# Second and third feed-forward of a two-layer diffusion backbone: third chunk of four inner tiles, projected by seven block products

## The chip, the core and the metric

One core of one Trainium2 chip runs the whole inference step as one program. The metric is the device time of that program in microseconds (us); lower is better. Three runs of the kernel before took 2325.58, 2327.49 and 2329.98 us; the median is 2327.49 us.

## The reference

640 token rows (512 latent ones, 128 context ones) of width 1024 go through two layers. Each layer is a feed-forward, a mixer and a second feed-forward, all in float32:

```python
def ffn_sub(x, g, shift, scale, gate, w_in, w_out):
    h = modulate(rms_norm(x, g), shift, scale)
    a, b = jnp.split(h @ w_in, 2, axis=-1)
    return x + gate * (FFN_RESIDUAL * ((jax.nn.silu(a) * b) @ w_out))
```

The inner width is 2816, which is 22 tiles of 128. `shift`, `scale` and `gate` come from `silu(c) @ w_mod + b_mod`, a product of one vector for each of the two token groups with a 1024 by 9216 matrix for each layer. The mixer of layer 0 holds pooling and neighbourhood attention, that of layer 1 grouped-query attention.

## The kernel before

Activations are kept transposed: `x[m]`, m = 0 to 7, holds 128 of the 1024 features by 640 tokens. Tokens are handled in two groups of 320 (`G`). There are four feed-forwards, `ffn(l, j)`; their index 2l+j picks an entry of `CHUNKS`. "First" to "fourth" below are these four in order.

**Exact products.** A float32 product is made of three matmuls of rounded parts: high by high, high by low, low by high. Each weight tile read from memory into `raw` (four buffers) is split by `split_w` (L106 and L107): ACT rounds it into `whi`, DVE writes the rest into `wlo` (five buffers of each). Activations are split in the same way (`hid`, `hhi` and `hlo`). So a weight tile costs PE three matmuls of 320 columns for each token group, and costs ACT and DVE one pass each.

**Input projection.** For most of the 22 inner tiles, `product_set` (from L512) forms the two halves of `h @ w_in` by seven block products instead of eight: 7 products of 4 feature tiles with 3 matmuls each, 84 matmuls of 320 columns at L128. It needs sums and differences of weight blocks, written by DVE (`s1` at L524, and L527 to L529), and three `split_w` and one `split_half` for each inner tile. `hidden7` (L611 to L620) turns the products into the gated inner tile: DVE at L615, L617, L618, L619, and the split at L609. L615 needs the sixth of the seven products, so 12 matmuls of the set are left when it may start.

**Output projection.** Inner tiles are taken in chunks. In the first three feed-forwards the chunks are 6, 6, 5 and 5 tiles. For a chunk of n tiles and each m, one weight tile of 128 x 128n is loaded and split, PE runs n x 3 x 2 matmuls (L136, L137, L139), and DVE adds the gated result to `x[m]` (`gate_add`, L402: one piece of 320, and one of 192 and one of 128, since the two token groups have their own gates). The fourth feed-forward has chunks of 4, 4, 4, 4 and 6; the first four of them go through `out_set` (from L668): two values of m at a time, 2 x 2 blocks, seven block products (L690) of two tiles with three matmuls each, 42 matmuls where 48 stand otherwise. DVE forms four sums of weight blocks for this (L676 to L679), splits 768 and 1024 columns, and adds `w5` twice (L715, L719); ACT copies four intermediate results (L694, L704). Its inner tiles are prepared by `hid_split`: the first two of a chunk are kept as `hk` (half a tile, split) and as `kept`, the other two are split in full, and with each of them two further combinations (L599 to L601, and two more splits at L609).

**Filler.** The modulation vectors for later stages are computed on DVE in the first three feed-forwards, spread between the other work. One `mod_tile` (L157 to L163) loads a 512 KB row block of `w_mod` (`rawm`, from the pool of `raw`) and runs one multiply-and-sum over 1024 columns for each of the two token groups (L161, custom DVE instruction, with a short read of the accumulator behind it). Its elementwise result is not needed; it goes to `junk`, a bf16 tile of its own. `filler(1)` follows each m of a chunk that isn't the last, and `fill_set` puts one tile or none behind an input projection.

**Order.** In the feed-forwards the instructions of each engine are put in a fixed order when the program is built; pools say how many buffers a tile has, and a tile waits for the release of the buffer that it takes. Each engine runs its list in that order. All loads go through one queue, SP's.

Of the kernel before, what the change touches and what calls it, by code (L numbers as in the profile page):

```python
# [6 lines left out]
F32 = mybir.dt.float32  # L7
F32R = mybir.dt.float32r
BF16 = mybir.dt.bfloat16
AF = mybir.ActivationFunctionType  # L10
ALU = mybir.AluOpType
# [4 lines left out]
P, D, KT = 128, 1024, 8  # L16
NT, G = 640, 320
NFT = 22
CHUNKS = ((6, 6, 5, 5),) * 3 + ((4, 4, 4, 4, 6),)
SEVEN = 3  # L20
NCONV = (5, 4, 4, 4)
EPS = 1e-6
WINDOWS = (2, 4, 8, 16)
# [9 lines left out]
def grp(a, g):  # L33
    return a[:, g * G:(g + 1) * G]
# [7 lines left out]
class Body:  # L42
    def __init__(self, nc, tc, ctx, i, o):
        self.nc, self.tc, self.i, self.o = nc, tc, i, o
        self.n = 0
        self.behind = None
        self.pend, self.hold, self.chains, self.hf, self.front = None, None, [], None, None
        k = self.keep = self.pool(ctx, "keep", 1)
        self.raw = self.pool(ctx, "raw", 4)
        self.wr = self.pool(ctx, "wr", 5)  # L50
        self.hp = self.pool(ctx, "hp", 1)
        self.tp = self.pool(ctx, "tp", 5)
        self.x = [k.tile([P, NT], F32, name=f"x{m}") for m in range(KT)]
        self.mod = k.tile([P, 2, 2, 9, KT], F32, name="mod")
        self.acol = k.tile([P, 2, 2, 3, KT], F32, name="acol")
        self.bmod = k.tile([P, 2, 9, KT], F32, name="bmod")
        self.gn = k.tile([P, 7, KT], F32, name="gn")
        self.cst = k.tile([P, 640], F32, name="cst")
        self.anti = self.cst[:, 512:640]
        self.ident = self.cst[:, 0:128]  # L60
        self.bones = self.cst[:, 128:256]
        self.sel = self.cst[:, 256:352]
        self.edge = self.cst[:, 352:380]
        self.ones = self.cst[:, 384:512]
# [77 lines left out]
    def mod_begin(self, ctx):  # L142
        nc, i = self.nc, self.i
        p = self.modp = self.pool(ctx, "modp", 1)
        self.sil = p.tile([P, 2, D], F32, name="sil")
        self.junk = p.tile([P, D], BF16, name="junk")

    def mod_load(self):
        nc, i = self.nc, self.i
# [6 lines left out]
    def mod_tile(self, l, v, f):  # L156
        nc = self.nc  # L157
        r = self.raw.tile([P, 1024], F32, tag="raw", name=self.nm("rawm"))
        nc.sync.dma_start(out=r, in_=self.i["wmT"][l, v * KT + f])
        for q in range(2):  # L160
            nc.vector.tensor_tensor_reduce(out=self.junk, in0=r, in1=self.sil[:, q], op0=ALU.mult, op1=ALU.add,  # L161
                                           scale=1.0, scalar=0.0, accum_out=self.mod[:, q, l, v, f:f + 1])
        if f == KT - 1:  # L163
            self.mod_done(l, v)
# [13 lines left out]
    def start_first(self, pool):  # L178

        nc, i = self.nc, self.i  # L180
# [17 lines left out]
        def wm_load(f):  # L198
            wms[f] = [pool.tile([P, 4, 256], F32, tag="wm", bufs=NWM, name=self.nm("wm")) for _ in range(2)]
            for half in range(2):  # L200
                nc.sync.dma_start(out=wms[f][half], in_=i["wm0"][f, half])

        wm_load(0)
        for c in (slice(0, 384), slice(512, 640)):
            nc.sync.dma_start(out=self.cst[:, c], in_=i["cst"][:, c])
        for t, n in ((self.gn, "gn"), (self.bmod, "bmod")):
            nc.sync.dma_start(out=t, in_=i[n])
        w = [self.load_w(i["w_in"][0, 0, 0, 0])]
# [54 lines left out]
        p = [[self.bank() for _ in range(2)] for _ in range(3)]  # L263
# [293 lines left out]
    def ffn(self, ctx, l, j, nxt, fill=(), first=False):  # L557

        nc = self.nc
        fill = list(fill)  # L560
        nconv = NCONV[2 * l + j]
        chunks, seven = CHUNKS[2 * l + j], 2 * l + j == SEVEN
        pairs, kept = {}, {}
        early = 4
        spread = max(0, len(fill) - (32 if first else 28))
# [3 lines left out]
        hp = self.pool(ctx, "hid", 7)  # L569
# [12 lines left out]
            return hid_split(sl, f)  # L582

        def hid_split(sl, f):
            if not seven or f >= NFT - chunks[-1]:
                return split_full(sl)
            k = f % 4
            b11, b12 = grp(sl, 0), grp(sl, 1)
            if k < 2:
                half = hp.tile([P, 2, G], F32R, tag="hk", bufs=3, name=self.nm("hk"))  # L590
                nc.scalar.activation(half[:, 0], b11, AF.Copy)
                nc.vector.tensor_tensor(half[:, 1], b11, half[:, 0].bitcast(F32), op=ALU.subtract)
                nc.vector.tensor_tensor(b11, b12, b11, op=ALU.subtract)
                kept[f] = sl
                return half[:, 0], half[:, 1]
            h2 = split_full(sl)
            t = kept.pop(f - 2)
            t1, t3, t4, t2 = grp(t, 0), grp(t, 1), b11, b12
            nc.vector.tensor_tensor(t3, b12, t3, op=ALU.subtract)  # L599
            nc.vector.tensor_tensor(t2, b12, t1, op=ALU.subtract)  # L600
            nc.vector.tensor_tensor(t4, b11, t2, op=ALU.subtract)  # L601
            pairs[f] = h2, split_full(t), split_full(sl)
            return h2

        def split_full(sl):
            hid = hp.tile([P, 2, NT], F32R, tag="hid", name=self.nm("hid"))
            hi, lo = hid[:, 0], hid[:, 1]
            nc.scalar.activation(hi, sl, AF.Copy)
            nc.vector.tensor_tensor(lo, sl, hi.bitcast(F32), op=ALU.subtract)  # L609
            return hi, lo  # L610
# [41 lines left out]
        while len(hid) < nconv:  # L652
            p = []
# [12 lines left out]
        def inproj(f):  # L666
            hid.append(hidden7(f, *self.product_set([win[l, j, f, ab] for ab in range(2)])))
            fill_set(f)  # L668
# [58 lines left out]
        for c, n in enumerate(chunks):  # L727
            last = c == len(chunks) - 1
            while len(hid) < min(NFT, f0 + n + 1):
                inproj(len(hid))  # L730
            ht = hid[f0:f0 + n]
            wc = wout[l, j, f0 * P * D:(f0 + n) * P * D].rearrange("(m p x) -> m p x", m=KT, p=P)
            hk = lambda k, g: (grp(ht[k][0], g), grp(ht[k][1], g))
            if seven and not last:
                behind = None
                for m in range(0, KT, 2):
                    step = out_set(wc[m], wc[m + 1], m, f0)
                    for k in range(3):
                        if behind:
                            next(behind)  # L740
                        next(step)
                    if behind:
                        next(behind)
                    behind = step
                for _ in behind:
                    pass
            elif not last:
                for m in range(KT):
                    w, p = self.unit(wc[m]), [self.bank() for _ in range(2)]
                    for k in range(n):  # L750
                        self.mm3([p[g][:, :G] for g in range(2)], w, k, [hk(k, g) for g in range(2)],
                                 k == 0, k == n - 1)
                    for g in range(2):
                        self.gate_add(m, g, p[g], l, v)
                    filler(1)
            else:
                while fill:
                    filler(1)
                self.norm_begin()

                def out_one(w, m, g):
                    p = self.bank()
                    for k in range(n):
                        self.mm3([p[:, :G]], w, k, [hk(k, g)], k == 0, k == n - 1)
                    self.gate_add(m, g, p, l, v)
                    self.norm_add(m, g)

                for mh in range(2):
                    ws = [self.unit(wc[m]) for m in range(4 * mh, 4 * mh + 4)]
                    for g in range(2):  # L770
                        for u in range(4):
                            out_one(ws[u], 4 * mh + u, g)
                            if mh == 1 and g == 1:
                                self.norm_part(u, nxt)
                self.norm_last(nxt)
            f0 += n
# [258 lines left out]
    def mixer0(self, ctx, nxt):  # L1035
        nc, i = self.nc, self.i
        l = 0
# [88 lines left out]
        with ExitStack() as ca:  # L1126
            bp = self.pool(ca, "b", 1)
# [3 lines left out]
                    nc.gpsimd.memset(b[:, c:c + P], 0.0)  # L1131
            msk = bp.tile([P, 7, 16], F32, name="msk")
            nc.sync.dma_start(out=msk, in_=i["mask"])

            rbs = {}

# [7 lines left out]
            def bias_turn(head, turn):  # L1144

                rb = rbs[head]
                nc.tensor.matmul(turn[:, 0:265], self.anti, rb[:, 0:265], start=True, stop=True)
                nc.scalar.copy(rb[:, 0:265], turn[:, 0:265])


# [459 lines left out]
def layout(a):  # L1610
# [16 lines left out]
    parts = []  # L1627
    for j, chunks in enumerate(CHUNKS):
        for c, n in enumerate(chunks):
# [57 lines left out]
```

## Time and profile before

| | us |
|---|---|
| median of three runs | 2327.49 |
| the profiled execution, its own time | 2330.14 |
| its span in the profile | 2328.4 |
| PE busy / PE weight loads busy | 2282.6 / 2207.7 |
| DVE busy | 1973.6 |
| ACT busy | 1166.6 |
| SP's queue from the second feed-forward's first weights of the third chunk to its last | 993.28 to 1031.94 |
| the same in the third feed-forward | 1429.59 to 1468.13 |

How to read it: busy time of an engine is the time in which at least one of its instructions is recorded; matmuls overlap in the pipeline, so the duration of one matmul (309 ns on average for 320 columns) is longer than the distance at which the next one follows. Where a part of the program costs time is read from the start of one instruction to the start of the next. A row such as "DVE wlo L107 <- ACT whi L106" names an idle time of DVE ahead of L107 and what ended it.

### The profile page before, as it was taken

What the parts mean: (1) busy time and instruction counts of PE and PEld (TensorE: products, weight loads), DVE (VectorE), ACT (ScalarE), POOL (GpSimd) and SP (SyncE); (2) the same over time, 40 slices, a digit from 0 to 9 for tenths busy, and PEclk for the clock granted to TensorE, in tenths of its full rate; (3) what the DMA queues carried; (4) which work ended last, traced back from release to release, by engine and by line L of the source; (5) the groups of instructions that cost most, each with busy time, mean ns of one, the idle gap of its engine ahead of it and who ended that gap; (6) DMA issues with size and microseconds to landing.
All of it is one profiled execution on the core that took longest, in us unless ns stands there. A gap on an engine that the chain in (4) does not pass through costs nothing.

```text
span 2328.4 us, 40561 instructions
## 1 busy us (share of the span) xinstructions
PE 2282.6 (98%) x15854; PEld 2207.7 (95%) x15854; DVE 1973.6 (85%) x3955; ACT 1166.6 (50%) x2153; POOL 2.2 (0%) x10
## 2 busy tenths in 40 slices
PE   8999999999999999999999999999999999999998
PEld 5999999998889999999999999998888889999997
DVE  6999989695889989787799887969888888999875
ACT  5525253463666434334552525347766665555552
POOL 0000000000000000000000000000000000000000
PEclk9999999999999999999999999999999999999999
DMA  7353544332111434343225253432101002223221
GB/s 296 118 189 127 183 140 160 119 108 87 49 47 55 163 127 148 115 154 117 93 89 183 98 183 111 161 100 74 48 28 37 28 28 72 76 90 96 77 96 60
DMA packets 82096, 252.27 MB, mean 108 GB/s; under 512 B 9712, under 2 KB 15728, under 8 KB 81904
## 3 DMA queue, kind: packets, MB, share of 16 engines
q1 hardware_dynamic: 81904, 249.67, 32.6%
q8 instruction: 125, 2.05, 0.4%
q14 instruction: 67, 0.55, 0.1%
HBM read 246.23 MB, written 3.41 MB: 107 GB/s over the span
## 4 chain that ended last, share of the span: by engine, by line
PE 81%; DVE 12%; ACT 3%; DMA 3%; issue 2%; SPq 0%; DVEq 0%; ACTq 0%
PE mm L128 30%; PE mm L136 13%; PE mm L137 12%; PE mm L139 12%; PE mm L690 4%; DVE wlo L107 2%; PE tr L824 2%; PE pv L1462 2%; DVE junk L161 1%; DMA rawm<-in_wmT 1%; PE sc L1427 1%; DVE x L402 1%; DVE g L344 1%; DVE hlo L350 1%; PE pv L1227 1%
## 5 line engine op out<-in xcount | busy, mean ns | idle before, releaser
L106 ACT ACTIVATE whi<-raw 128x1024 fp32r<-128x1024 f32 (+2 forms) x427 | 417.6, 986 | 461.1 <-PE mm L137 174.3
L107 DVE TENSOR_TENSOR wlo<-raw,whi 128x1024 fp32r<-128x1024 f32 (+2 forms) x427 | 479.7, 1130 | 74.8 <-ACT whi L106 74.0
L128 PE MATMUL mm<-hhi,whi 128*128 128x320 f32 x1136 | 350.9, 309 | 0.0
L128 PE MATMUL mm<-hhi,wlo 128*128 128x320 f32 x1136 | 350.9, 309 | 0.0
L128 PE MATMUL mm<-hlo,whi 128*128 128x320 f32 x1136 | 350.5, 309 | 0.0
L136 PE MATMUL mm<-hid,whi 128*128 128x320 f32 x1152 | 350.2, 310 | 0.0
L137 PE MATMUL mm<-hid,whi 128*128 128x320 f32 x1152 | 349.0, 309 | 0.0
L161 DVE CUSTOM_DVE_ANT_0 junk<-rawm,sil 128x1024 bf16<-128x1024 f32 x256 | 312.4, 1221 | 24.7 <-DMA rawm<-in_wmT 19.9
L139 PE MATMUL mm<-hid,wlo 128*128 128x320 f32 x1152 | 289.2, 309 | 0.0
L136 PE MATMUL mm<-hhi,whi 128*128 128x320 f32 x896 | 276.2, 320 | 6.4 <-ACT hhi L347 5.6
L137 PE MATMUL mm<-hlo,whi 128*128 128x320 f32 x896 | 275.0, 313 | 1.1 <-DVE hlo L350 1.1
L402 DVE SCALAR_TENSOR_TENSOR x<-mm,mod,x 128x320 f32<-128x320 f32 (+2 forms) x536 | 216.0, 440 | 65.9 <-PE mm L139 64.5
L139 PE MATMUL mm<-hhi,wlo 128*128 128x320 f32 x896 | 248.1, 311 | 2.8 <-DVE wlo L107 2.8
L137 PEld LDWEIGHTS mm<-hid,whi 128*128 128x128 f32 x1152 | 216.2, 188 | 0.7
L136 PEld LDWEIGHTS mm<-hid,whi 128*128 128x128 f32 x1152 | 216.2, 188 | 0.7
L128 PEld LDWEIGHTS mm<-hlo,whi 128*128 128x128 f32 x1136 | 213.3, 188 | 0.0
L128 PEld LDWEIGHTS mm<-hhi,wlo 128*128 128x128 f32 x1136 | 213.3, 188 | 0.0
L128 PEld LDWEIGHTS mm<-hhi,whi 128*128 128x128 f32 x1136 | 213.2, 188 | 0.0
L139 PEld LDWEIGHTS mm<-hid,wlo 128*128 128x128 f32 x1152 | 199.2, 188 | 0.0
L136 PEld LDWEIGHTS mm<-hhi,whi 128*128 128x128 f32 x896 | 166.9, 189 | 15.6 <-ACT hhi L347 9.1
L128 PE MATMUL mm<-Th,whi 128*128 128x320 f32 x568 | 176.1, 310 | 3.0 <-ACT mm L537 3.0
L128 PE MATMUL mm<-Th,wlo 128*128 128x320 f32 x568 | 175.3, 309 | 0.0
(252 smaller groups left out, 4511.6 us busy)
## 6 DMA issues: line engine op xcount, KB each, us to landing
raw<-in_w_in SPq DMA_DIRECT2D x176, 512.0 KB, 3.9
rawm<-in_wmT SPq DMA_DIRECT2D x128, 512.0 KB, 3.7
raw<-in_w_out SPq DMA_DIRECT2D x56, 384.0 KB, 3.4
raw<-in_w_out SPq DMA_DIRECT2D x48, 320.0 KB, 2.9
wm<-in_wm SPq DMA_DIRECT2D x16, 512.0 KB, 10.2
raw<-in_w_out SPq DMA_DIRECT2D x32, 256.0 KB, 2.9
raw<-in_w_ab SPq DMA_DIRECT2D x12, 512.0 KB, 3.8
raw<-in_w_c SPq DMA_DIRECT2D x10, 512.0 KB, 3.5
```

Source lines behind the costliest of these rows:

```text
L106: a = (nc.scalar.activation(hi[:, c], r[:, c], AF.Copy), nc.vector.tensor_tensor(lo[:, c], r[:, c], hi[:, c].bitcast(F32), op=ALU.subtract))
L107: nc.vector.tensor_tensor(lo[:, c], r[:, c], hi[:, c].bitcast(F32), op=ALU.subtract))
L128: nc.tensor.matmul(out, a[:, c], b, start=start and first, stop=last, skip_group_check=True)
L136: nc.tensor.matmul(out, hi[:, c], rh, start=start, stop=False)
L137: nc.tensor.matmul(out, hi[:, c], rl, start=False, stop=False)
L139: nc.tensor.matmul(out, lo[:, c], rh, start=False, stop=stop)
L161: nc.vector.tensor_tensor_reduce(out=self.junk, in0=r, in1=self.sil[:, q], op0=ALU.mult, op1=ALU.add, scale=1.0, scalar=0.0, accum_out=sel ...
L344: nc.vector.scalar_tensor_tensor(out=t[:, c], in0=x[:, c], scalar=self.acol[:, q, l, s, m:m + 1], in1=rstd[:, c], op0=ALU.mult, op1=ALU.mult)
L402: a = nc.vector.scalar_tensor_tensor(out=x[:, c], in0=ps[:, c], scalar=self.mod[:, q, l, v, m:m + 1], in1=x[:, c], op0=ALU.mult, op1=ALU.add)
L690: nc.tensor.matmul(p, a[:, c], b, start=start and first, stop=last, skip_group_check=True)
L824: self.nc.tensor.transpose(ps[:, a * P:(a + 1) * P], src[:, b * P:(b + 1) * P], self.ident)
L1462: nc.tensor.matmul(st["pv"][64 * f:64 * f + 64, ti * P:(ti + 1) * P], V[:, (4, 0, 1, 2, 3)[a], vc], rhs, start=a == 0, stop=a == 4)
```

## The change

The second and third feed-forwards take chunks of 6, 6, 4 and 6 inner tiles. Their third chunk goes through `hid_split`'s preparation and `out_set`, as the chunks of the fourth feed-forward did before. `filler(2)` stands behind each pair of m there, in place of `filler(1)` behind each m; the number of modulation tiles is as before. The first and the fourth feed-forward keep their chunks.

Room in memory for the two `hk` buffers comes from two places. `junk` is no tile of its own any more: each `mod_tile` takes the one buffer of the tag `s1`, which `product_set` uses for its sum of weight blocks. And the reversed unit matrix `anti`, 128 columns of the constants, is loaded in the mixer of layer 0, where it is used, and not at the start.

```diff
-CHUNKS = ((6, 6, 5, 5),) * 3 + ((4, 4, 4, 4, 6),)
-SEVEN = 3
+CHUNKS = ((6, 6, 5, 5), (6, 6, 4, 6), (6, 6, 4, 6), (4, 4, 4, 4, 6))
+SEVEN = ((), (2,), (2,), (0, 1, 2, 3))
...
-        self.cst = k.tile([P, 640], F32, name="cst")
-        self.anti = self.cst[:, 512:640]
+        self.cst = k.tile([P, 512], F32, name="cst")
...
         self.sil = p.tile([P, 2, D], F32, name="sil")
-        self.junk = p.tile([P, D], BF16, name="junk")
...
         nc.sync.dma_start(out=r, in_=self.i["wmT"][l, v * KT + f])
+        junk = self.raw.tile([P, 512], F32, tag="s1", bufs=1, name=self.nm("junk")).bitcast(BF16)
         for q in range(2):
-            nc.vector.tensor_tensor_reduce(out=self.junk, in0=r, in1=self.sil[:, q], op0=ALU.mult, op1=ALU.add,
+            nc.vector.tensor_tensor_reduce(out=junk, in0=r, in1=self.sil[:, q], op0=ALU.mult, op1=ALU.add,
...
-        for c in (slice(0, 384), slice(512, 640)):
-            nc.sync.dma_start(out=self.cst[:, c], in_=i["cst"][:, c])
+        nc.sync.dma_start(out=self.cst[:, 0:384], in_=i["cst"][:, 0:384])
...
-        chunks, seven = CHUNKS[2 * l + j], 2 * l + j == SEVEN
+        chunks, seven = CHUNKS[2 * l + j], SEVEN[2 * l + j]
+        place = {sum(chunks[:c]) + k: k for c in seven for k in range(4)}
...
         def hid_split(sl, f):
-            if not seven or f >= NFT - chunks[-1]:
+            if f not in place:
                 return split_full(sl)
-            k = f % 4
+            k = place[f]
...
-                half = hp.tile([P, 2, G], F32R, tag="hk", bufs=3, name=self.nm("hk"))
+                half = hp.tile([P, 2, G], F32R, tag="hk", bufs=3 if len(seven) > 1 else 2, name=self.nm("hk"))
...
-            if seven and not last:
+            if c in seven:
                 behind = None
                 for m in range(0, KT, 2):
                     step = out_set(wc[m], wc[m + 1], m, f0)
...
                     behind = step
+                    filler(2)
                 for _ in behind:
                     pass
...
             nc.sync.dma_start(out=msk, in_=i["mask"])
+            anti = bp.tile([P, P], F32, name="anti")
+            nc.sync.dma_start(out=anti, in_=i["cst"][:, 512:640])
...
-                nc.tensor.matmul(turn[:, 0:265], self.anti, rb[:, 0:265], start=True, stop=True)
+                nc.tensor.matmul(turn[:, 0:265], anti, rb[:, 0:265], start=True, stop=True)
```

In the second feed-forward the third chunk is projected when inner tile 16 (counted from 0) has been formed, and before tile 17: one tile earlier than before, since the chunk is one tile shorter. The places below are on DVE. Line numbers of the changed kernel are one or two lower than those of the kernel before (L160 for L161, L106 for L107, L400 for L402, L522 for L524).

In the middle of the second feed-forward's third chunk, before: the work of one m. `x` is what the projection is added to, `junk,mod<-rawm,sil` is modulation's filler, `wlo` a weight split.

```order
L402 SCALAR_TENSOR_TENSOR x_72<-mm_11276,mod,x_72 128x320
L402 SCALAR_TENSOR_TENSOR x_72<-mm_11277,mod,x_72 128x192
L402 SCALAR_TENSOR_TENSOR x_72<-mm_11277,mod,x_72 128x128
L107 TENSOR_TENSOR wlo_11502<-raw_11499,whi_11501 128x640
L161 ISA junk,mod<-rawm_11540,sil 128x1024
```

The same place now, in the work of one pair of m; the four rows of `raw` are the sums of weight blocks.

```order
L675 TENSOR_TENSOR raw_11297<-raw_11296 128x256
L677 TENSOR_TENSOR raw_11297<-raw_11296 128x256
L676 TENSOR_TENSOR raw_11297<-raw_11297,raw_11296 128x256
L106 TENSOR_TENSOR wlo_11305<-raw_11296,whi_11304 128x768
L678 TENSOR_TENSOR raw_11297<-raw_11296,raw_11297 128x256
L714 TENSOR_TENSOR g_11327<-mm_11247,g_11249 128x320
L400 SCALAR_TENSOR_TENSOR x_73<-mm_11325,mod,x_73 128x320
L400 SCALAR_TENSOR_TENSOR x_73<-g_11327,mod,x_73 128x192
L106 TENSOR_TENSOR wlo_11309<-raw_11297,whi_11308 128x1024
```

A pair of m has four sums, two larger splits and two additions of `w5` (L714, L718) in place of two splits of 640 columns; the gate additions and the filler are as many as before.

The end of the same chunk, before: `s` is the sum with which the weights of the next inner tile begin, `slo` the low part of its split; `x_74` and `x_75` belong to m = 4 and 5.

```order
L524 TENSOR_TENSOR s_1795_11548<-raw_11546 128x512
L107 TENSOR_TENSOR wlo_11551<-raw_11544,whi_11550 128x1024
L118 TENSOR_TENSOR slo_11555<-s_1795_11548,shi_11554 128x512
L527 TENSOR_TENSOR raw_11546<-raw_11544,raw_11546 128x512
L402 SCALAR_TENSOR_TENSOR x_74<-mm_11370,mod,x_74 128x320
L402 SCALAR_TENSOR_TENSOR x_74<-mm_11371,mod,x_74 128x192
L402 SCALAR_TENSOR_TENSOR x_74<-mm_11371,mod,x_74 128x128
L528 TENSOR_TENSOR raw_11544<-s_1795_11548,raw_11544 128x512
L161 ISA junk,mod<-rawm_11674,sil 128x1024
```

And now, behind the last filler of the chunk:

```order
L718 TENSOR_TENSOR g_11427<-mm_11444,g_11427 128x320
L400 SCALAR_TENSOR_TENSOR x_77<-mm_11476,mod,x_77 128x320
L400 SCALAR_TENSOR_TENSOR x_76<-g_11427,mod,x_76 128x192
L400 SCALAR_TENSOR_TENSOR x_76<-g_11427,mod,x_76 128x128
L522 TENSOR_TENSOR s_1876_11502<-raw_11500 128x512
L525 TENSOR_TENSOR raw_11500<-raw_11498,raw_11500 128x512
L117 TENSOR_TENSOR slo_11509<-s_1876_11502,shi_11508 128x512
L526 TENSOR_TENSOR raw_11498<-s_1876_11502,raw_11498 128x512
L527 TENSOR_TENSOR raw_11498<-raw_11498 128x512
```

Before, the next tile's sums stood four m ahead of the end, with filler behind them; now they stand behind all gate additions and all filler of the chunk.

## The prediction

> **What bounds the kernel now.** I read the page's busy times first, then busy times by stretch of the second and third feed-forward, then the waits of PE there, then the timelines of DVE and ACT in the third chunk of the second feed-forward.
>
> ```profile
> span 2328.4 us, 40561 instructions
> PE 2282.6 (98%) x15854; PEld 2207.7 (95%) x15854; DVE 1973.6 (85%) x3955; ACT 1166.6 (50%) x2153; POOL 2.2 (0%) x10
> ```
>
> ```profile
> core 0: us, PE busy (x) PEld busy (x) DVE busy (x) ACT busy (x) POOL busy (x), PEclk, DMA share, GB/s
> 725.00:1550.00 825.00, 823.87 (x5608) 821.92 (x5607) 706.95 (x1181) 364.04 (x596) 0.00 (x0) 1.00 0.40 129
> 1023.95:1060.00 36.05, 36.05 (x248) 36.05 (x247) 35.68 (x67) 9.06 (x12) 0.00 (x0) 1.00 0.56 180
> ```
>
> ```profile
> PE mm L128 <- ACT mm L537: 1.1, 3, 0.7
> ```
>
> From 725 to 1550 us PE is busy for 823.87 of 825 us and waits 1.1 us in all. So the end is set by PE, and every matmul taken out is worth its distance to the next one, as long as nothing new makes PE wait. The second stretch is the old third chunk: there DVE is busy for 35.68 of 36.05 us. The share of 85% over the span hides that DVE is full in just this place.
>
> The price of a matmul: ACT's weight splits in that chunk are released by PE, once for each m.
>
> ```profile
> 1028.18 0.74 ACT L106 ACTIVATE whi<-raw 128x640 fp32r<-128x640 f32 x1 [1.04 <-PE mm L137]
> 1032.58 0.74 ACT L106 ACTIVATE whi<-raw 128x640 fp32r<-128x640 f32 x1 [3.66 <-PE mm L137]
> 1036.98 0.74 ACT L106 ACTIVATE whi<-raw 128x640 fp32r<-128x640 f32 x1 [3.66 <-PE mm L137]
> ```
>
> They follow each other at 4.40 us, the time of 5 x 3 x 2 = 30 matmuls: 0.1467 us each.
>
> **The change: PE.** The old third and fourth chunk have 8 x (5 + 5) x 6 = 480 matmuls. The new ones have 4 pairs x 42 = 168 and 8 x 6 x 6 = 288, together 456. That is 24 fewer in each of two feed-forwards, 48 x 0.1467 = **7.0 us less** of PE. (PE's instruction lists say the same: 15246 matmuls before, 15198 now, so the change does what it says.) The third chunk itself shrinks from 240 x 0.1467 = 35.2 us to 168 x 0.1467 = 24.6 us of PE.
>
> **The change: DVE.** The same chunk on DVE, one m of the kernel before:
>
> ```profile
> 1031.83 1.22 DVE L161 CUSTOM_DVE_ANT_0 junk<-rawm,sil 128x1024 bf16<-128x1024 f32 x1
> 1032.97 0.08 DVE L161 DVE_READ_ACCUMULATOR2_ANT mod<- 128x1 f32 x1
> 1033.09 1.23 DVE L161 CUSTOM_DVE_ANT_0 junk<-rawm,sil 128x1024 bf16<-128x1024 f32 x1
> 1034.24 0.08 DVE L161 DVE_READ_ACCUMULATOR2_ANT mod<- 128x1 f32 x1
> 1034.24 1.13 DVE L402 SCALAR_TENSOR_TENSOR x<-mm,mod,x 128x320 f32<-128x320 f32 x3
> 1035.28 0.82 DVE L107 TENSOR_TENSOR wlo<-raw,whi 128x640 fp32r<-128x640 f32 x1
> 1036.02 1.22 DVE L161 CUSTOM_DVE_ANT_0 junk<-rawm,sil 128x1024 bf16<-128x1024 f32 x1
> ```
>
> From start to start, a filler half (L161) takes 1.15 us, the three gate additions 1.04, a split of 640 columns 0.74; one m takes 1036.02 - 1031.83 = 4.19 us, against 4.40 on PE. So it just fitted. The other operations, from the same timeline and from the fourth feed-forward, where block products run already:
>
> ```profile
> 1043.66 0.68 DVE L524 TENSOR_TENSOR s<-raw 128x512 f32<-128x512 f32 x1
> 1044.26 1.22 DVE L107 TENSOR_TENSOR wlo<-raw,whi 128x1024 fp32r<-128x1024 f32 x1
> 1045.40 0.68 DVE L118 TENSOR_TENSOR slo<-s,shi 128x512 fp32r<-128x512 f32 x1
> ```
>
> ```profile
> 1957.11 0.82 DVE L609 TENSOR_TENSOR hid<-t,hid 128x640 fp32r<-128x640 f32 x1
> 1957.84 0.42 DVE L678 TENSOR_TENSOR raw<-raw 128x256 f32<-128x256 f32 x1
> ...
> 1965.99 0.95 DVE L107 TENSOR_TENSOR wlo<-raw,whi 128x768 fp32r<-128x768 f32 x1
> 1966.86 0.49 DVE L592 TENSOR_TENSOR hk<-t,hk 128x320 fp32r<-128x320 f32 x1
> 1967.26 0.42 DVE L676 TENSOR_TENSOR raw<-raw 128x256 f32<-128x256 f32 x1
> 1967.59 0.49 DVE L593 TENSOR_TENSOR t<-t 128x320 f32<-128x320 f32 x1
> ...
> 1983.21 0.48 DVE L715 TENSOR_TENSOR g<-mm,g 128x320 f32<-128x320 f32 x1
> 1983.61 0.68 DVE L118 TENSOR_TENSOR slo<-s,shi 128x512 fp32r<-128x512 f32 x1
> ```
>
> Start to start: 0.60 for 512 columns, 1.14 for a split of 1024, 0.87 for 768, 0.73 for 640, 0.33 for a sum of 256, 0.40 for 320. One pair of m now costs DVE 4 x 0.33 + 0.87 + 1.14 + 2 x 0.40 + 2 x 1.04 + 4 x 1.15 = 10.8 us, of which 4.6 is filler; PE needs 42 x 0.1467 = 6.2. Four pairs are 43 us of DVE beside 24.6 of PE. Without the filler it would be 25 beside 24.6, which is why the fourth feed-forward, with the same block products and no filler, doesn't stall.
>
> Can DVE work ahead, or put the filler off? Ahead: hardly. The in-projection before the chunk takes PE 12.3 us, seen by L615 of two successive tiles:
>
> ```profile
> 997.15 0.49 DVE L615 TENSOR_TENSOR g<-mm,g 128x320 f32<-128x320 f32 x1 [1.34 <-PE mm L128]
> ...
> 1009.45 0.49 DVE L615 TENSOR_TENSOR g<-mm,g 128x320 f32<-128x320 f32 x1 [1.34 <-PE mm L128]
> ```
>
> DVE was 1.34 us ahead there. In the changed order the DVE rows between the L615 of tiles 14 and 15, and of 15 and 16, sum to 12.5 and 12.4 us with the durations above (the two further combinations and splits of tiles 14 and 15 are in them): no lead is gained. Off: no. The weights of tile 17 begin with `s1`, whose one buffer the filler's `junk` now takes too. So `s1` comes behind all eight filler tiles of the chunk, and in DVE's list it stands behind the last gate addition; before, it stood four m ahead of the end.
>
> So I count how late DVE is. Start: L615 of tile 16, which can't run before PE's sixth product of that tile. End: the split (L107) of `w2`, the third weight operand of tile 17, without which PE can't go on. The DVE rows between, in the second feed-forward: 13 filler halves 15.0; gate additions 8 x 1.04 = 8.3; L715 and L719 8 x 0.40 = 3.2; splits for pairs 2 to 4 3 x 2.01 = 6.0; ten sums 3.3; tile 16's own 4 x 0.40 + 0.73 = 2.3; tile 17's two splits and five operations of 512 columns 5.3; two such for tile 18 1.2; small ones 0.5. Sum 45.1 us. PE has 12 matmuls of tile 16, 168 of the chunk and 32 of tile 17 to do in that time: 212 x 0.1467 = 31.1 us. **PE waits 14.0 us.** In the third feed-forward the list gives 45.5 us, and 204 matmuls ahead of the same point, 29.9 us: **15.6 us**. Behind it DVE's rows come to 10 to 12.3 us for each tile, so it keeps up, but what PE lost isn't given back. Within the chunk the wait falls in parts: about 2 us before pair 3's split, 5 before pair 4's, the rest before `s1` and `w2` of tile 17.
>
> **The change: the rest.** ACT was busy for 9.06 of 36.05 us in the old chunk and has room for its copies: nothing. SP's queue: the load of the next pair's `raw` waits for a buffer that the split of this pair frees, with the filler's two loads behind it. DVE's waits for `rawm` bound that from both sides:
>
> ```profile
> DVE junk L161 <- DMA rawm<-in_wmT: 15.3, 16, 2.4
> ```
>
> 15.3 us in 16 waits over 825 us, at most 2.4 at once; in the new chunk more than 8 us of DVE work lies between the freeing of a buffer and the use of what is loaded into it, except for tile 17's first tile, so 0 to 2.4 us for each feed-forward; I take 0. `anti` stands in the queue ahead of the two loads (`rb`) for which its matmul waits as well:
>
> ```profile
> PE mm L1147 <- DMA rb<-in_rpb: 0.4, 1, 0.4
> ```
>
> so 0, and at most 0.4 us. `junk` in `s1`'s buffer also ties the filler of each tile to the weights of the next in the first feed-forward, without more work. PE's waits between 40 and 450 us, in the kernel before:
>
> ```profile
> PE mm L128 <- ACT mm L537: 1.4, 2, 1.0
> ```
>
> I bound the change of these 1.4 us by 0 and twice their amount, 3 us, and take 0. The sum: -7.0 + 14.0 + 15.6 = **+22.6 us**. The profiled execution took 2330.14 us (span 2328.4), 2.65 above the median of 2327.49; 2352.7 there is 2350.1 on the scale of the runs.
>
> **Rivals.** *PE's saving alone.* PE has 98% and DVE 85%; if pools and list let DVE catch up, 7.0 us go and nothing comes back: 2320.5. It decides where the stretch from L615 to `w2` is under 31 us, that is if the 15.0 us of filler fell outside it. For it speaks that PE never waited for DVE in 825 us; against it, that DVE was full at 35.68 of 36.05 and is given more in less time. [...]
>
> *Half of it hidden.* If L161 with its output in another buffer, or some of the sums, run shorter, or PE finds other matmuls in its list, half of the wait remains: -7.0 + 14.8 = +7.8, 2335.3.
>
> *The clock falls behind the waits.* A stretch with one wait of 2.17 us:
>
> ```profile
> 706.83 1.08 PE L136 MATMUL mm<-hhi,whi 128*128 128x320 f32 x4 [2.17 <-ACT hhi L347]
> ```
>
> ```profile
> 700.00:725.00 25.00, 22.38 (x134) 20.94 (x134) 23.77 (x56) 15.43 (x31) 0.00 (x0) 0.93 0.19 64
> ```
>
> There the granted clock was 0.93 over 25 us, 1.75 us of matmul time lost. Only the last wait in each chunk has matmuls behind it that nothing else delays, so 2 x 1.75 = 3.5 us more: 2353.6. [...]
>
> *DVE's own waits on top.* 2.4 us for a load and as much for PE's results in both chunks, 3 in the first feed-forward and the clock: +22.6 + 9.6 + 3 + 3.5 = +38.7, 2366.
>
> **Numbers.** Forecast 2350: 0.50. Clock: 0.24. DVE's waits on top: 0.10. Half hidden: 0.08. Saving alone: 0.08. The range leaves out the saving and the upper part of the last-named waits: 2335 to 2362. A measurement of this kernel tells 0.2% (4.7 us) from no change: faster 0.08; within it 0.04, the lower part of the half hidden case; slower 0.88.
>
> **What would show it.** Right: in the third chunks of the second and third feed-forward PE waits for DVE at `wlo` of `out_set` and at `slo` and `wlo` of tile 17, 13 to 17 us in each, with DVE at 98% or more for some 45 us from L615 of tile 16 on. Wrong: PE without waits there and a span about 7 us shorter; or the time lost at other places, such as the first feed-forward, the mixer's `anti` or DVE waiting for `rawm`.

## The result and the profile after

| | before | after |
|---|---|---|
| median, us (lowest to highest; runs) | 2327.93 (2325.58 to 2329.98; 4) | 2351.79 (2350.45 to 2352.5; 4) |
| span of the profiled execution, us | 2328.4 | 2349.6 |

The changed kernel is slower: 23.9 us, ratio 1.0102 with a 95% interval of 1.009 to 1.0113.

The first lines of the page of after:

```profile
span 2349.6 us, 40562 instructions
PE 2285.4 (97%) x15806; PEld 2210.9 (94%) x15806; DVE 2013.6 (86%) x4027; ACT 1189.7 (51%) x2193; POOL 2.2 (0%) x10
```

PE has 48 matmuls fewer than before and yet 2.8 us more of busy time. A matmul that runs longer counts as busy, so this line alone already says that idle time won't be all of the loss. Across the span DVE's share moves from 85 to 86%: one could not read the cause from it.

PE's waits of after from 1000 to 1080 us, around the third chunk of the second feed-forward (us in total, times, longest):

```profile
PE mm L689 <- DVE wlo L106: 5.1, 3, 3.0
PE mm L127 <- ACT shi L116: 3.9, 1, 3.9
PE mm L689 <- ACT whi L105: 0.6, 1, 0.6
PE mm L689 <- ACT mm L693: 0.4, 1, 0.4
PE mm L127 <- DVE slo L117: 0.2, 1, 0.2
```

They come to 10.2 us, where the kernel before had 1.1 us in all from 725 to 1550. L689 is the block product of `out_set`, L127 the first product of tile 17. `shi` is ACT's, but it is the rounding of `s1`, which DVE forms (L522): the wait names the last link, not the late engine. In the third feed-forward the same rows come to 10.6 us:

```profile
PE mm L689 <- DVE wlo L106: 5.8, 3, 3.2
PE mm L127 <- ACT shi L116: 4.6, 1, 4.6
PE mm L689 <- ACT mm L693: 0.2, 1, 0.2
```

Busy times of after by stretch. The first two rows run from L614 (L615 before) of tile 16 to L614 of tile 17, in the second and the third feed-forward; the other three are stretches of the second in which the clock column reads 0.50:

```profile
core 0: us, PE busy (x) PEld busy (x) DVE busy (x) ACT busy (x) POOL busy (x), PEclk, DMA share, GB/s
1008.89:1061.81 52.92, 42.72 (x249) 40.59 (x248) 52.10 (x103) 21.10 (x37) 0.00 (x0) 0.90 0.40 138
1456.18:1510.75 54.57, 43.93 (x255) 42.31 (x254) 53.15 (x105) 22.34 (x37) 0.00 (x0) 0.87 0.41 134
1027.52:1030.93 3.41, 3.41 (x15) 3.41 (x14) 3.41 (x8) 0.44 (x1) 0.00 (x0) 0.50 0.28 108
1037.76:1041.17 3.41, 3.01 (x12) 2.99 (x12) 3.41 (x8) 0.96 (x3) 0.00 (x0) 0.50 0.73 259
1051.41:1054.82 3.41, 3.28 (x12) 3.28 (x13) 3.34 (x6) 1.98 (x3) 0.00 (x0) 0.50 0.00 0
```

Without waits such a stretch would take PE 168 matmuls of the chunk and 84 of one input projection, 24.6 + 12.3 = 36.9 us. It takes 52.92 and 54.57: 16.0 and 17.7 us are lost. DVE is busy for 98.5 and 97.4% of the two. The clock column gives the second part of the loss: each of the three short stretches follows a wait, and half of the time in which PE is "busy" there is lost to the slow clock: 0.50 x 3.41, 0.50 x 3.01 and 0.50 x 3.28 are 1.7, 1.5 and 1.6 us, 4.8 together. 10.2 idle and 4.8 of clock make 15.0 us. In the third feed-forward two such stretches (3.41 us each at 0.50, from 1474.67 and 1484.91, with PE busy for 3.41 and 3.19 us) lose 1.7 and 1.6 us, and a longer one at 0.50, of which 5.0 us lie behind PE's start at 1496.98, loses 2.5: 5.8 of clock and 10.6 idle make 16.4. About 1 us of each loss is in neither.

The end of the stretch on DVE, from the last filler on:

```profile
1008.89 0.49 DVE L614 TENSOR_TENSOR g<-mm,g 128x320 f32<-128x320 f32 x1
...
1046.22 1.22 DVE L160 CUSTOM_DVE_ANT_0 junk<-rawm,sil 128x1024 bf16<-128x1024 f32 x1
...
1049.40 0.69 DVE L522 TENSOR_TENSOR s<-raw 128x512 f32<-128x512 f32 x1
...
1050.79 0.69 DVE L117 TENSOR_TENSOR slo<-s,shi 128x512 fp32r<-128x512 f32 x1
...
1054.06 3.49 DVE L106 TENSOR_TENSOR wlo<-raw,whi 128x1024 fp32r<-128x1024 f32 x3
```

The first of the three splits at 1054.06 is that of `w2`; by the distance of 1.14 us it ends at 1055.2, 46.3 us behind L614 of tile 16. PE at the same place:

```profile
1050.81 0.41 PE L127 MATMUL mm<-Th,shi 128*128 128x320 f32 x1 [3.87 <-ACT shi L116]
...
1051.97 0.47 PE L127 MATMUL mm<-Th,shi 128*128 128x320 f32 x1
1052.24 0.47 PE L127 MATMUL mm<-Tl,shi 128*128 128x320 f32 x1
...
1055.75 0.31 PE L127 MATMUL mm<-Th,wlo 128*128 128x320 f32 x1
```

PE starts again 1.4 us behind DVE's start on `s1`, and 1.2 us later its matmuls follow at 0.27 us instead of 0.1467. `Th,wlo` at 1055.75, 0.55 us behind the end of the split, is the first one on `w2`'s low part. No wait is recorded there: the slow matmuls fill the time in which DVE gets there.

### The profile page after: what moved, and what is told of

Read it like the earlier page. It is cut to its first block, busy times and chain, and to the rows that moved or that the text cites. A ratio compares the mean times of both kernels' runs of the same rounds, so it can differ in the third digit from the quotient of the medians.

```text
span 2349.6 us, 40562 instructions
## 1 busy us (share of the span) xinstructions
PE 2285.4 (97%) x15806; PEld 2210.9 (94%) x15806; DVE 2013.6 (86%) x4027; ACT 1189.7 (51%) x2193; POOL 2.2 (0%) x10
## 3 DMA queue, kind: packets, MB, share of 16 engines
HBM read 246.23 MB, written 3.41 MB: 106 GB/s over the span
## 4 chain that ended last, share of the span: by engine, by line
PE 86%; DVE 9%; ACT 2%; issue 2%; DMA 1%; SPq 0%; DVEq 0%; ACTq 0%
PE mm L127 35%; PE mm L135 13%; PE mm L136 12%; PE mm L138 12%; PE mm L689 5%; PE tr L824 2%; PE pv L1464 2%; DVE junk L160 1%; PE sc L1429 1%; DVE x L400 1%; DVE wlo L106 1%; PE pv L1229 1%; DVE hlo L348 1%; DVE g L342 1%; DVE t L298 1%
## 5 line engine op out<-in xcount | busy, mean ns | idle before, releaser
L105 ACT ACTIVATE whi<-raw 128x1024 fp32r<-128x1024 f32 (+2 forms) x427 | 423.8, 1000 | 457.3 <-PE mm L136 156.6
L106 DVE TENSOR_TENSOR wlo<-raw,whi 128x1024 fp32r<-128x1024 f32 (+2 forms) x427 | 486.8, 1146 | 59.3 <-ACT whi L105 57.5
L127 PE MATMUL mm<-hhi,wlo 128*128 128x320 f32 x1136 | 351.5, 309 | 0.0
L127 PE MATMUL mm<-hhi,whi 128*128 128x320 f32 x1136 | 351.4, 309 | 0.0
L127 PE MATMUL mm<-hlo,whi 128*128 128x320 f32 x1136 | 350.9, 309 | 0.0
L160 DVE CUSTOM_DVE_ANT_0 junk<-rawm,sil 128x1024 bf16<-128x1024 f32 x256 | 312.8, 1222 | 6.1 <-ACT sil L152 2.5
L135 PE MATMUL mm<-hid,whi 128*128 128x320 f32 x1024 | 311.5, 310 | 0.0
L136 PE MATMUL mm<-hid,whi 128*128 128x320 f32 x1024 | 310.8, 308 | 0.0
L400 DVE SCALAR_TENSOR_TENSOR x<-mm,mod,x 128x320 f32<-128x320 f32 (+2 forms) x504 | 207.1, 446 | 86.9 <-PE mm L138 85.2
L138 PE MATMUL mm<-hid,wlo 128*128 128x320 f32 x1024 | 262.9, 309 | 0.0
L127 PEld LDWEIGHTS mm<-hhi,wlo 128*128 128x128 f32 x1136 | 213.8, 188 | 0.0
L127 PEld LDWEIGHTS mm<-hhi,whi 128*128 128x128 f32 x1136 | 213.8, 188 | 0.0
L127 PEld LDWEIGHTS mm<-hlo,whi 128*128 128x128 f32 x1136 | 213.7, 188 | 0.0
L136 PEld LDWEIGHTS mm<-hid,whi 128*128 128x128 f32 x1024 | 192.2, 188 | 0.6
L135 PEld LDWEIGHTS mm<-hid,whi 128*128 128x128 f32 x1024 | 192.1, 188 | 0.4
L138 PEld LDWEIGHTS mm<-hid,wlo 128*128 128x128 f32 x1024 | 178.6, 188 | 0.0
L127 PE MATMUL mm<-Th,whi 128*128 128x320 f32 x568 | 175.4, 309 | 1.0 <-ACT mm L535 1.0
L127 PE MATMUL mm<-Tl,whi 128*128 128x320 f32 x568 | 175.3, 309 | 0.0
```

The costliest lines, as they stand in the source:

```text
L105: a = (nc.scalar.activation(hi[:, c], r[:, c], AF.Copy), nc.vector.tensor_tensor(lo[:, c], r[:, c], hi[:, c].bitcast(F32), op=ALU.subtract))
L106: nc.vector.tensor_tensor(lo[:, c], r[:, c], hi[:, c].bitcast(F32), op=ALU.subtract))
L127: nc.tensor.matmul(out, a[:, c], b, start=start and first, stop=last, skip_group_check=True)
L135: nc.tensor.matmul(out, hi[:, c], rh, start=start, stop=False)
L136: nc.tensor.matmul(out, hi[:, c], rl, start=False, stop=False)
L138: nc.tensor.matmul(out, lo[:, c], rh, start=False, stop=stop)
```

## The experiments

The theory under test: DVE is late in the two third chunks because the eight filler tiles stand inside them; the block products by themselves fit. The rivals: the block products' own DVE work (sums, larger splits, `w5`) is the overload; or the new places of `junk` and `anti` are. The table has all runs; differences are against the kernel before, as the same chip ran it (2327.93 for after, 2327.80 for the next four, 2328.09 for the others).

| kernel | median, us | difference | ratio (95%) |
|---|---|---|---|
| after | 2351.79 | +23.9 | 1.0102 (1.009 to 1.0113) |
| after, filler moved to the last chunk | 2318.47 | -9.3 | 0.9957 (0.9945 to 0.997) |
| after, memory moves alone | 2325.69 | -2.1 | 0.9989 (0.998 to 0.9998) |
| before, filler doubled in the third chunk | 2351.23 | +23.4 | 1.0096 (1.0081 to 1.0111) |
| after, `junk` in a buffer of `t` | 2385.54 | +57.7 | 1.0241 (1.0227 to 1.0255) |
| filler moved, first feed-forward too | 2321.01 | -7.1 | 0.9964 (0.9951 to 0.9976) |
| half of the filler moved | 2338.60 | +10.5 | 1.0044 (1.0031 to 1.0058) |
| second feed-forward only | 2336.92 | +8.8 | 1.0037 (1.0024 to 1.0051) |
| before, filler moved, no block products | 2330.30 | +2.2 | 1.0008 (0.9999 to 1.0017) |

**The filler put off.** The changed kernel with no filler in the third chunk. Its eight tiles go to the last chunk, two behind each three of its steps:

```diff
                     behind = step
-                    filler(2)
...
-                while fill:
-                    filler(1)
+                late = iter(range(12))
...
                             out_one(ws[u], 4 * mh + u, g)
+                            if next(late, 2) % 3 < 2:
+                                filler(1)
```

> The changed kernel, with the eight filler tiles taken out of the third chunk of the second and third feed-forward and spread over the first twelve of the sixteen steps of the last chunk; all work is done. Theory (DVE overfull in the third chunk): a pair of m then costs DVE 10.8 - 4.6 = 6.2 us beside 6.2 on PE, so the waits of the chunk (10.2 and 10.6 us recorded) fall to at most 2 us in each, and the 7.0 us of matmuls are kept: about 2321 us, 2319 to 2327. The last chunk has 42 us of PE for 18.4 us more of DVE and should not wait more than 2 us. Rival (the block products themselves, or junk in the buffer of s1, make PE wait): the waits stay and the time is 2340 or more.

2318.47 us: faster than both kernels. PE's waits from 725 to 1560 us are one row, and the stretch between the two L614 is 37.71 us in the second feed-forward, all of it PE (37.70 in the third):

```profile
PE mm L135 <- ACT hid L607: 1.2, 2, 0.9
```

```profile
core 0: us, PE busy (x) PEld busy (x) DVE busy (x) ACT busy (x) POOL busy (x), PEclk, DMA share, GB/s
1006.22:1043.93 37.71, 37.71 (x259) 37.71 (x258) 36.40 (x69) 22.07 (x37) 0.00 (x0) 1.00 0.31 99
```

So the place of the filler costs 2351.79 - 2318.47 = 33.3 us. The block products' own DVE work fits: DVE is at 97% there, and PE doesn't wait. It fits with little to spare: the 0.8 us above 36.9 are DVE's, whose L614 of tile 16 waited 0.7 us for PE, while that of tile 17 came straight behind a filler tile. The first rival falls.

**The memory moves alone.** The chunks as before; `junk` in `s1`'s buffer and `anti` loaded late remain:

```diff
-CHUNKS = ((6, 6, 5, 5), (6, 6, 4, 6), (6, 6, 4, 6), (4, 4, 4, 4, 6))
-SEVEN = ((), (2,), (2,), (0, 1, 2, 3))
+CHUNKS = ((6, 6, 5, 5),) * 3 + ((4, 4, 4, 4, 6),)
+SEVEN = ((), (), (), (0, 1, 2, 3))
```

> The kernel before with only the two memory moves of the change: junk in the buffer of s1, and anti loaded in the mixer. Chunks and block products as before. Theory: no more work on any engine and no shorter stretch for it, so 2328 us, at most 3 us more. Rival (the shared buffer holds the next tile's s1 back behind the filler, and that is what costs): most of the 24 us, 2340 to 2352.

2325.69 us. The moves cost nothing; they gain about 2 us (0.5 to 4.7 by the interval). Which of the two gains it was not separated. Of the waits of the kernel before, over the whole span, most of PE's for L537 went, shown here as before has it and then as this kernel has it (L535 there):

```profile
PE mm L128 <- ACT mm L537: 3.0, 7, 1.0
```

```profile
PE mm L127 <- ACT mm L535: 0.7, 2, 0.5
```

The second rival falls, as far as the moves by themselves go. The gain and the saving on PE add up, within the intervals, to what the kernel with the filler put off shows: -7.0 - 2.1 = -9.1 against -9.3.

**The filler doubled without block products.** The kernel before, with the second chunk's filler moved into the third, so that DVE is overloaded there and nothing else changes:

```diff
-                    filler(1)
+                    filler(1 if first or c == 0 else 2 * c - 2)
```

> The kernel before, without any block product added, but with the eight filler tiles of the second chunk of the second and third feed-forward moved to their third chunk (two behind each m, none in the second chunk). Theory (too much DVE work in that stretch is the cause, whatever it is): one m costs DVE 4.19 + 2.3 = 6.5 us beside 4.40 on PE; from L615 to L615 over the chunk 42.1 + 18.4 = 60.5 us beside 47.5, so PE waits about 13 us in each of two places: 2354 us, 2340 to 2360. Rival (block products, their seeding or their four sums are the cause): 2328 us.

2351.23 us. With PE's old 240 matmuls in the chunk and 16 filler tiles instead of 8, PE waits at the same kind of places, from 725 to 1600 us:

```profile
PE mm L128 <- ACT whi L106: 5.7, 2, 2.9
PE mm L128 <- ACT shi L117: 3.2, 1, 3.2
PE mm L139 <- DVE wlo L107: 2.4, 1, 2.4
...
```

and the granted clock behind them is 0.90 and 0.83 over 25 us:

```profile
core 0: us, PE busy (x) PEld busy (x) DVE busy (x) ACT busy (x) POOL busy (x), PEclk, DMA share, GB/s
1025.00:1050.00 25.00, 25.00 (x173) 25.00 (x172) 24.82 (x53) 2.96 (x4) 0.00 (x0) 1.00 0.58 186
1050.00:1075.00 25.00, 17.87 (x102) 16.43 (x101) 23.24 (x43) 6.68 (x9) 0.00 (x0) 0.90 0.49 160
1075.00:1100.00 25.00, 24.49 (x143) 24.09 (x143) 21.47 (x32) 11.81 (x19) 0.00 (x0) 0.83 0.42 138
```

All but one of the larger waits stand behind the chunk, at the weights of the next inner tiles; the one of L139 stands inside it, in the third feed-forward. No block product is needed for the loss: too much DVE work in a stretch is enough.

**`junk` in another buffer.** This was to show whether the chunk also stalls when the filler doesn't share `s1`'s buffer:

```diff
-        junk = self.raw.tile([P, 512], F32, tag="s1", bufs=1, name=self.nm("junk")).bitcast(BF16)
+        junk = self.t()[:, 0:512].bitcast(BF16)
```

> The changed kernel, with junk in one of the five buffers of t in place of the buffer of s1, so that s1 of the next inner tile does not wait for the filler. Theory (the amount of DVE work decides): 2352 us, within 5. Rival (the shared buffer): 2321 to 2338.

2385.54 us, far from every theory. The buffers of `t` are those in which inner tiles are formed, so the filler now stands in line with these, in all feed-forwards. PE's longest waits over the whole span, L535 being the copies of `product_set`:

```profile
PE mm L689 <- DVE wlo L106: 12.6, 7, 3.5
PE mm L127 <- ACT mm L535: 10.5, 13, 1.2
PE mm L127 <- ACT shi L116: 9.8, 4, 3.2
```

The time doesn't separate what it was meant to: the run puts a larger dependence in the place of the one it removes. The order on DVE does say something. Here, in the second feed-forward, `s1` stands behind all filler of the chunk although the filler has another buffer:

```profile
1067.36 1.22 DVE L160 CUSTOM_DVE_ANT_0 t<-rawm,sil 128x1024 bf16<-128x1024 f32 x1
...
1070.35 0.68 DVE L522 TENSOR_TENSOR s<-raw 128x512 f32<-128x512 f32 x1
```

And with the memory moves alone, where the two share the buffer, `s1` stands four m ahead of the end, with filler behind it, as in the kernel before:

```profile
1041.72 0.68 DVE L522 TENSOR_TENSOR s<-raw 128x512 f32<-128x512 f32 x1
...
1047.03 1.22 DVE L160 CUSTOM_DVE_ANT_0 junk<-rawm,sil 128x1024 bf16<-128x1024 f32 x1
```

So the shared buffer is neither needed for the late place of `s1` nor enough for it. `junk` in a tile of its own wasn't tried with the new chunks, since there is no room for it.

**Half of the filler.** The kernel with the filler put off, with `filler(1)` restored behind each pair, so that four tiles stand in the third chunk and four in the last:

```diff
                     behind = step
+                    filler(1)
```

> The changed kernel with half of the third chunk's filler (four tiles, one behind each pair of m) and the other four tiles in the last chunk. Theory (lateness is the sum of DVE work less PE work): the stretch from L614 of tile 16 to that of tile 17 was 52.92 and 54.57 us beside 36.9 without waits; it falls by 4 x 2.3 = 9.2 us each, to 6.8 and 8.5 us of wait. With 7.0 for the matmuls and 2.1 for the memory moves: 2328 + 15.3 - 9.1 = 2334 us, 2329 to 2339. Rival (a threshold, such as the order of s1 behind any filler): near 2352 or near 2318.

2338.60 us, at the slow end of what was expected. From L614 to L614:

```profile
core 0: us, PE busy (x) PEld busy (x) DVE busy (x) ACT busy (x) POOL busy (x), PEclk, DMA share, GB/s
1009.12:1056.05 46.93, 42.07 (x257) 40.46 (x257) 43.64 (x86) 21.24 (x37) 0.00 (x0) 0.93 0.35 113
1449.92:1496.23 46.31, 40.87 (x259) 39.25 (x258) 43.94 (x87) 21.28 (x37) 0.00 (x0) 0.96 0.35 114
```

With no, four and eight filler tiles in the chunk the stretch is 37.7, 46.9 and 52.9 us in the second feed-forward and 37.7, 46.3 and 54.6 in the third. Four tiles are 9.2 us of DVE, and the first four already cost about that much: at 97% there was no slack to take them. The next four cost 6.0 and 8.3. With four, DVE itself stands idle for 3.3 and 2.4 us of the stretch, so its work isn't the whole of the time there. DVE's recorded waits in the two stretches are for ACT's rounding of weights (`whi`, 1.6 and 1.7 us), for ACT's copy at L693 (1.3 us, in the second alone) and for PE (0.2 and 0.5 us). Why ACT is late there was not followed further.

**The second feed-forward only.** The third has its chunks of before:

```diff
-CHUNKS = ((6, 6, 5, 5), (6, 6, 4, 6), (6, 6, 4, 6), (4, 4, 4, 4, 6))
-SEVEN = ((), (2,), (2,), (0, 1, 2, 3))
+CHUNKS = ((6, 6, 5, 5), (6, 6, 4, 6), (6, 6, 5, 5), (4, 4, 4, 4, 6))
+SEVEN = ((), (2,), (), (0, 1, 2, 3))
```

> The changed kernel with the new third chunk in the second feed-forward alone; the third one has chunks of 6, 6, 5 and 5 as before. Theory (each place costs its own wait): 16.0 us of wait, 3.5 for matmuls and 2.1 for the memory moves: 2338 us, 2334 to 2342. Rival (one cause for both, such as the constants or the shared buffer): 2328 or 2352.

2336.92 us. PE's two largest waits from 725 to 1140 us are those of after to 0.1 us (9.4 us in all, against 10.2); from 1140 to 1580 it has none:

```profile
PE mm L689 <- DVE wlo L106: 5.0, 3, 3.0
PE mm L127 <- ACT shi L116: 3.9, 1, 3.9
```

The loss is made in each feed-forward by itself: -2.1 - 3.5 + 16.0 = +10.4 for the second alone, +8.8 measured (5.6 to 11.9 by the interval).

**The filler put off, no block products.** The kernel before with the third chunk's filler moved to the last chunk:

```diff
-                    filler(1)
+                    filler(c < 2 or first)
...
-                while fill:
-                    filler(1)
+                late = iter(range(12))
...
                             out_one(ws[u], 4 * mh + u, g)
+                            if next(late, 2) % 3 < 2:
+                                filler(1)
```

> The kernel before, with the eight filler tiles of the third chunk of the second and third feed-forward moved to the last chunk, and nothing else: no block products, junk in its own tile. Theory (PE did not wait for DVE there, so freeing DVE gives nothing): 2328 us, 2325 to 2330. Rival (the late filler itself is what made the kernel with late filler faster): 2319 to 2322.

2330.30 us, no difference that can be measured. So the 9.3 us above are not the filler's new place as such: that place only makes room for the block products.

**The first feed-forward too.** The filler put off in all three, and the chunks of 6, 6, 4 and 6 in the first as well (`row` comes from another pool to make room):

```diff
-CHUNKS = ((6, 6, 5, 5), (6, 6, 4, 6), (6, 6, 4, 6), (4, 4, 4, 4, 6))
-SEVEN = ((), (2,), (2,), (0, 1, 2, 3))
+CHUNKS = ((6, 6, 4, 6),) * 3 + ((4, 4, 4, 4, 6),)
+SEVEN = ((2,),) * 3 + ((0, 1, 2, 3),)
```

> As the kernel with the filler moved late (2318.5 us), and the first feed-forward takes the same chunks, with block products in its third chunk and its eight filler tiles in the last one; room comes from a tile of the start that is now given back early. Theory (matmuls count where DVE fits): 24 matmuls, 3.5 us less: 2315 us, 2312 to 2319. Rival (DVE, at 46 to 49 of 50 us in the first feed-forward, is overfull there): as much filler in its last chunk and in-projections makes PE wait, 2319 or more.

2321.01 us: no gain over the kernel with two. Another 3.5 us of matmuls are gone, and PE loses as much in the first feed-forward. This kernel in one stretch at its end (PE, PE weight loads, DVE, ACT and POOL busy, clock, DMA):

```profile
450.00:475.00 25.00, 22.51 (x151) 21.96 (x150) 22.99 (x44) 11.04 (x18) 0.00 (x0) 1.00 0.64 206
```

and the kernel without it at the same time:

```profile
450.00:475.00 25.00, 25.00 (x168) 24.47 (x167) 19.77 (x42) 12.60 (x21) 0.00 (x0) 1.00 0.36 114
```

The two programs are some microseconds apart there, so the rows show that PE loses time, 2.5 us in this stretch with DVE busy for 22.99 us instead of 19.77, but not by which instruction. PE's recorded waits name it: from 30 to 480 us this kernel has 2.4 us for ACT's copies at L535, 1.4 for `t` of DVE's L298 and 1.1 for `wlo`, 4.9 in all, and the kernel without the first feed-forward's block products has none.

## Why the prediction was right, point by point

**PE's saving, -7.0 us: right.** The page has the 48 matmuls less, and where nothing delays them the kernel gains what the count says (-9.1 worked out with the memory moves, -9.3 measured).

**DVE's 10.8 us a pair against PE's 6.2, with 4.6 of filler: right.** The 768 column splits of pairs 3 and 4 start 11.2 us apart in the second feed-forward of after and 10.8 in the third. Without the filler 25 us stood beside 24.6; the run without it shows DVE at 97% and no waits. This closeness was the step on which most hung, and it is the one that the run of the filler put off tested.

**The stretch on DVE, 45.1 and 45.5 us: a little too small.** 46.3 us in both. In the third, L614 starts at 1456.18, and the first split of the row

```profile
1501.30 2.35 DVE L106 TENSOR_TENSOR wlo<-raw,whi 128x1024 fp32r<-128x1024 f32 x2
```

ends 1.14 behind its start, at 1502.4. DVE is busy for 45.53 of the 46.31 us and for 45.40 of the 46.26; the 0.8 and 0.9 us of idle time between, which a sum of distances doesn't hold, are most of the 1.2 us more in the second and all of the 0.8 in the third. By these lengths PE's wait is 46.3 - 31.1 = 15.2 and 46.3 - 29.9 = 16.4 us; up to L614 of tile 17 it is 16.0 and 17.7, against 14.0 and 15.6 forecast. Of that difference of 4.1 us, 2.0 are the longer stretches, and the rest comes behind the split of `w2`.

**The form of the wait: in part.** It stood where it was expected, at `wlo` of `out_set` and at the first weights of tile 17. But "13 to 17 us in each" of waits is not what the rows have: they have 10.2 and 10.6. A third of the loss is PE at a granted clock of 0.50. The parts in the second feed-forward, as this view of PE's timeline shows them:

```profile
1025.45 0.41 PE L689 MATMUL mm<-hk,wlo 128*128 128x320 f32 x1 [2.96 <-DVE wlo L106]
...
1026.87 1.51 PE L689 MATMUL mm<-hid,whi 128*128 128x320 f32 x6 [0.58 <-ACT whi L105]
...
1036.64 0.41 PE L689 MATMUL mm<-hk,wlo 128*128 128x320 f32 x1 [1.73 <-DVE wlo L106]
```

Pair 3: 3.5 us idle (forecast 2). Pair 4: 1.7 idle and 0.4 more inside it (the third of the three waits of 5.1 us above), and the 1.7 of slow clock behind pair 3's wait in front of it (forecast 5). Tile 17: 4.1 idle and 1.5 and 1.6 of clock (forecast 7). The forecast counted the time correctly as DVE's, and took all of it for idle time of PE.

**The rival of the clock: it was there, at half of its price at most.** It stood at 1.75 us for each chunk, on the ground that behind the last wait nothing else delays the matmuls. That ground failed: the slow matmuls behind the wait for `s1` ran while DVE still had `w2` to split. PE came to `w2` 0.55 us behind the split's end in the second feed-forward, and 0.45 in the third (1502.87 against 1502.4). This is the most the clock can have cost there; at the two waits inside the chunk of the second feed-forward PE came 0.15 us behind the split's end, counted the same way (1024.43 + 0.87 against 1025.45, 1035.62 + 0.87 against 1036.64). Behind these two waits the clock cost little, because DVE was late again: PE waited another 1.73 us at pair 4 and 3.87 us at tile 17. One place is open: in the third feed-forward DVE's gate addition at 1489.24 waited 0.75 us for a block product, just behind the stretch at 0.50 from 1484.91 to 1488.32, and part of that may be the clock's.

**The memory moves, taken at 0 with 0 to 3 us for the first feed-forward: mis-sized.** They gain 2.1 us. Tied to this is the argument that the filler can't be put off because `s1` shares its buffer with `junk`. The order is as described, but the reason given for it is wrong: `s1` stands behind all filler with `junk` in another buffer too, and with the moves alone it stands ahead of the last filler tile although they share one. What puts `s1` there stays open. Moving the filler in the program removes the loss with the buffer shared as it is.

**DVE's waits on top (2366): no.** Its waits for loads of the filler all but went, in after from 725 to 1600 us

```profile
DVE junk L160 <- DMA rawm<-in_wmT: 0.2, 1, 0.2
```

where before had 15.3 us (725 to 1550). This isn't because DVE is late: with the memory moves alone these waits come to 0.6 us. **PE's saving alone (2320.5): no**, for this order. PE's 98% and DVE's 85% over the span spoke for it; the row of the old chunk, with DVE busy for 35.68 of 36.05 us, spoke against it, and the measurement decides for the row. The 2320.5 describe well the kernel with the filler put off, at 2318.47.

**The sum.** -7.0 of matmuls, +33.7 of delay and -2.1 of the moves are +24.6; the runs have +23.9, the forecast had +22.6. Against the 37.7 us that the two stretches took without filler, the delay is 32.1 us and the sum +23.0. That the forecast came within 1.3 us is in part luck: it had the delay 4.1 us too small and left out the 2.1 us that the moves gain. The step that carries it, DVE's work against PE's in the chunk, is borne out by itself.

## What to carry to other kernels

Taking matmuls out of a stretch also takes away cover: a stretch that PE bounds by a few per cent is handed to the next engine, and its load must be recounted for the new length, in that stretch and not over the span. Where such an engine carries work that isn't due yet, move it to a stretch with slack in the same edit; here this is the difference between +23.9 and -9.3 us. When a wait is recorded for a helper's output (`shi` on ACT), follow it one step further back to the engine that is late.

## What the runs showed of the hardware

After waits of 3.0, 1.7 and 3.9 us (the second feed-forward of after) the granted clock fell to 0.50, but not at once: PE started again at 1025.45, 1036.64 and 1050.81, and by the clock column the slow stretches begin at 1027.52, 1037.76 and 1051.41, which is 2.1, 1.1 and 0.6 us later. Each of the three lasts 3.41 us. In the third feed-forward the clock was low as soon as PE started again behind 4.60 us of waiting: its column reads 1.00 from 1491.74 to 1495.15 and 0.50 from there to 1501.98, so it fell 1.8 us before PE's start. The runs don't show what sets the moment at which it falls.

```profile
1496.98 0.64 PE L127 MATMUL mm<-Th,shi 128*128 128x320 f32 x1 [4.60 <-ACT shi L116]
1497.41 0.47 PE L127 MATMUL mm<-Tl,shi 128*128 128x320 f32 x1
...
1501.68 0.45 PE L127 MATMUL mm<-Tl,shi 128*128 128x320 f32 x1
```

From the second of these rows to the third are 16 steps of 0.267 us; the slow stretch took 5.0 us of PE's time, up to 1501.98. Busy time hides this (from 1498.56 to 1501.98 PE is busy for all of 3.42 us); the clock column of a short stretch shows it.
